# A seven-product block scheme in f32: two of the seven products accumulated in PSUM onto banks of earlier products, in place of two VectorE additions per block pair

## The chip, the cores and the metric

The kernel runs on one core of one Trainium2 chip. The metric is the time of one execution on the device in microseconds (us): the median of three runs of the kernel before is 1294.61 (1294.13 to 1297.48). Lower is better.

## What is computed

One layer of a streaming encoder over 576 tokens (512 of a new stream, 64 of a running one), all in f32: model width 1024, FFN width 2816. What matters here are the matrix products; `W` stands for the weights of each.

```python
x += 0.5 * (silu(h @ W_gate) * (h @ W_up)) @ W_down      # h = rms_norm(x): first FFN, "f1"
p  = rms_norm(x) @ w_in                                  # 7 x 1024 columns
y_a = (B_a * dwconv3(C_a * V_a)) @ w_a_out
y_b = silu(layer_norm(dwconv31(glu(U_b)) + bias)) @ w_b_out
x += (sigmoid(g_a) * y_a + sigmoid(g_b) * y_b) @ w_out
x += 0.5 * (silu(h @ W_gate) * (h @ W_up)) @ W_down      # second FFN, "f2"
y  = rms_norm(x)
```

## The kernel before

**Products.** Tokens lie in the free dimension, in two halves of H = 288 columns. Each f32 operand is split into a high part (rounded to `float32r`) and a low part (the remainder), and a product is the sum of three matmuls: high x high, high x low, low x high. A matmul is 128x128 weights times 128x288 data into one PSUM bank.

**The block scheme.** From a certain column tile on (`PLAIN`: tile 4 of f1, tile 1 of f2; FFN tiles 0 to 21) gate and up are computed together, and so are two of the four pairs of column tiles of `w_b_out`. Such a *pair* is a 2x2 block product: two halves of the 1024 input rows and two column tiles on the weight side, two halves of the tokens and of the rows on the data side. Done plainly that is eight products of 128 columns by 512 rows by 288 tokens; the kernel does it in seven (a scheme of Strassen's kind), on sums and differences of weight halves and of data halves. Each product is 12 matmuls, `block` (L452): four row tiles, three parts each. The data forms are made once (`Forms.operands`, L669); the weight sums are made for each pair. The seven results q[0] to q[6] are then added up into gate and up, four halves in all. There are 41 pairs: 18 in f1, 2 in `w_b_out`, 21 in f2.

**Adding up, before** (`pair`, L863; the same in `block_pair`, L1240). After each product but the first one step is recorded:

```python
            steps = (
                lambda: sca.copy(q1, q[0]),
                lambda: dve.tensor_tensor(u2, q[1], q1, op=ALU.subtract),
                lambda: dve.tensor_tensor(u4, q[2], u2, op=ALU.subtract),
                q7,
                lambda: dve.tensor_tensor(half(t, 0), q[4], q1, op=ALU.add),
                gate,
            )
```

Here `q7` adds u3 = q[3] + u2 and writes the second up half, u3 - q[2]. `gate` adds the second gate half, q[5] + u4, multiplies by the norm's factor and takes ScalarE's SiLU. The last step, q[6] + u3, is recorded beside the next pair's first products. So a pair has one ScalarE copy out of PSUM and seven VectorE operations with a PSUM operand.

**Temporaries.** q1, q[0]'s copy, and u2 are the two halves of one temporary of 576 columns, u3 and u4 those of another (before). A temporary is one tile to the framework that sets the semaphores.

**PSUM.** Four tiles of two banks each (pool `mmps`, L135), 512 f32 to a bank. `bank()` (L164) hands out half a tile at a time, so that two consecutive products share a tile; the other users take whole tiles. A product writes 288 columns of its bank. The half that is left over is dropped at the end of each FFN group (L921) and after each `w_b_out` pair (L1273). Seven products before, five after the change: in both an odd number, so that a pair's first product falls on the first half of a tile in one pair and on the second half in the next.

**Order.** Every instruction is recorded at L88 in the order of the program, and each engine's queue keeps it. FFN column tiles come in four groups (`GROUPS`, L44: tiles 0-4, 5-9, 10-15, 16-21); after each group the down projection of that group's tiles follows. In between go the weight steps of `Stream` (L202), six units ahead of the product that needs them: a load on SyncE's queue, VectorE's sums of weight halves (`add`), ScalarE's high part (`begin`, L280), and the low part either on ScalarE and a GpSimd DMA that accumulates (L284) or by a VectorE subtraction (`end`). `ws.get` ahead of each product calls them, so they stand in the queues ahead of that product's step. In `block_pair` of tiles 6 and 7 the split of two merged tiles is recorded with the fourth step.

Of the kernel before, what the change touches and what calls it, by code (L numbers as in the profile page):

```python
# [13 lines left out]
ALU = mybir.AluOpType  # L14
# [8 lines left out]
KU = KT // 2  # L23
# [88 lines left out]
def tile_encoder_step(  # L112
# [707 lines left out]
    def ffn(f, xg, sums, finish, forms, R=None, todo=()):  # L820
# [42 lines left out]
        def pair(i, hs, last):  # L863
            qu, uu, t, cu = (ttile() for _ in range(4))
            q1, u2, u3, u4 = half(qu, 0), half(qu, 1), half(uu, 0), half(uu, 1)
            q = []

            def q7():
                dve.tensor_tensor(u3, q[3], u2, op=ALU.add)
                dve.tensor_tensor(half(cu, 1), u3, q[2], op=ALU.subtract)  # L870

            def gate():
                dve.tensor_tensor(half(t, 1), q[5], u4, op=ALU.add)
# [11 lines left out]
            for n, xs in enumerate(bs):  # L885
                q.append(block(ws.get(plan[f, "s", i][n]), xs))
                if n > 0:
                    steps[n - 1]()
                if rest:
                    rest.pop(0)()  # L890

            hs.append(None)
            at = len(hs) - 1

            def up():
                if last:
                    dve.tensor_tensor(t, t, R, op=ALU.mult)
                dve.tensor_tensor(half(cu, 0), q[6], u3, op=ALU.add)
# [341 lines left out]
    def block_pair(i):  # L1240
        j = 2 * i
        c1, c2, qu, uu = (ttile() for _ in range(4))
        q1, u2, u3, u4 = half(qu, 0), half(qu, 1), half(uu, 0), half(uu, 1)
        q = []

        def second():
            dve.tensor_tensor(u3, q[3], u2, op=ALU.add)
            dve.tensor_tensor(half(c2, 1), u3, q[2], op=ALU.subtract)

            if i == KU - 1:  # L1250
                MS[4], MS[5] = split(M[4]), split(M[5])

        def first():
            dve.tensor_tensor(half(c1, 1), q[5], u4, op=ALU.add)
# [3 lines left out]
        steps = (  # L1258
# [179 lines left out]
```

## Time and profile before

| | |
|---|---|
| median of three runs | 1294.61 us |
| span of the profiled execution | 1290.1 us |
| TensorE busy | 1279.4 us, 99% of the span, 9728 matmuls |
| VectorE busy | 925.1 us, 72% |
| ScalarE busy | 765.5 us, 59% |
| GpSimd busy | 361.6 us, 28% |
| TensorE's granted clock | 10 tenths in all but the last of the 40 slices |
| chain that ended last | 92% TensorE |

The times come from runs without the profiler's records, the rows from one profiled execution of 1290.1 us; what lies around its span makes the median longer. Rows of a stretch of time give the start and duration in us, the engine, the line, the operation with output and inputs by tile name, the shape, and in brackets how long the engine was idle before it and for whom. All of the kernel's engine instructions bear L88.

### The profile page before, as it was taken

The page shows a single profiled execution, that of the slowest core. Times are in us where ns is not written, and L with a number is a line of the kernel's source. Part 1 is how long each engine was busy: PE and PEld are TensorE (multiplying, and loading weights), DVE is VectorE, ACT ScalarE, POOL GpSimd, SP SyncE. Part 2 cuts the span into 40 slices and gives each one's busy share as a digit, 9 for nine tenths or more (in the row PEclk, how much of TensorE's full clock was granted, in tenths as well). Part 3 has the DMA queues.
Part 4 walks back from the last instruction along what each step waited for, and adds up shares of the span by engine and source line. Part 5 has one row for each costly group of instructions (what it writes and reads, how often), then busy time and mean ns, then how long its engine had stood idle before and what let it go on. Part 6 is the DMA issues. An engine that isn't in the chain of part 4 may idle for free.

```text
span 1290.1 us, 25702 instructions
## 1 busy us (share of the span) xinstructions
PE 1279.4 (99%) x9728; PEld 1277.5 (99%) x9728; DVE 925.1 (72%) x1539; ACT 765.5 (59%) x1359; POOL 361.6 (28%) x460
## 2 busy tenths in 40 slices
PE   9999999999999999999999999999999999999997
PEld 9999999999999999999999999999999999999997
DVE  6868668748846998888895166656867848847956
ACT  7655646646776645555444576477665655654664
POOL 0032332232333444333321221122142141241230
PEclk9999999999999999999999999999999999999998
DMA  7286787886799898788885767696687696796783
GB/s 220 70 181 154 163 180 155 177 181 149 154 224 232 174 200 173 165 172 174 172 172 124 163 142 154 151 236 145 139 175 171 151 197 151 164 204 138 158 172 97
DMA packets 286812, 215.26 MB, mean 167 GB/s; under 512 B 15456, under 2 KB 248928, under 8 KB 286688
## 3 DMA queue, kind: packets, MB, share of 16 engines
q0 software_dynamic: 56160, 92.43, 43.3%
q1 hardware_dynamic: 228784, 120.35, 32.8%
q8 instruction: 77, 1.26, 0.4%
q10 hardware_dynamic: 1744, 0.83, 0.2%
q14 instruction: 47, 0.39, 0.1%
HBM read 116.17 MB, written 4.98 MB: 94 GB/s over the span
## 4 chain that ended last, share of the span: by engine, by line
PE 92%; issue 4%; DVE 2%; DMA 1%; ACT 1%; POOL 0%; DVEq 0%; POOLq 0%; ACTq 0%
PE mm L88 92%; DVE tmp L88 0%; DMA g<-raw 0%; DMA raw<-in_w_b_out_dram 0%; DVE x L88 0%; DVE g L88 0%; DMA u<-raw 0%; ACT act L88 0%; DVE w L88 0%; POOL u L88 0%; DVE act L88 0%; ACT u L88 0%; ACT w L88 0%; ACT g L88 0%; POOL g L88 0%
## 5 line engine op out<-in xcount | busy, mean ns | idle before, releaser
L88 PE MATMUL mm<-act,u 128*128 128x288 f32 x4758 | 668.3, 293 | 0.1
L88 PEld LDWEIGHTS mm<-act,u 128*128 128x128 f32 x4758 | 638.9, 188 | 0.4 <-DMA u<-raw 0.3
L88 PE MATMUL mm<-act,g 128*128 128x288 f32 x3030 | 432.9, 294 | 0.9 <-DMA g<-raw 0.9
L88 PEld LDWEIGHTS mm<-act,g 128*128 128x128 f32 x3030 | 410.3, 188 | 1.1 <-DMA g<-raw 1.1
L88 POOL DMA_DIRECT2D u<-raw x197 | 172.3, 874 | 481.7 <-ACT u L88 317.4
L88 PE MATMUL mm<-act,act 128*128 128x288 f32 (+2 forms) x1896 | 259.9, 293 | 0.0
L88 PEld LDWEIGHTS mm<-act,act 128*128 128x128 f32 x1896 | 252.2, 188 | 0.5 <-ACT act L88 0.3
L88 ACT CAST u<-raw 128x512 fp32r<-128x512 f32 (+2 forms) x207 | 118.8, 574 | 172.0 <-PE mm L88 136.7
L88 POOL DMA_DIRECT2D g<-raw x126 | 109.9, 872 | 297.4 <-ACT g L88 242.7
L88 DVE SCALAR_TENSOR_TENSOR w<-g,prm,w 128x606 f32<-128x606 f32 x232 | 179.3, 844 | 1.4 <-ACT w L88 1.4
L88 DVE TENSOR_TENSOR tmp<-mm,tmp 128x288 f32<-128x288 f32 (+1 forms) x251 | 112.9, 459 | 70.3 <-PE mm L88 53.7
L88 ACT ACTIVATE u<-u 128x512 fp32r<-128x512 f32 (+2 forms) x197 | 116.8, 593 | 6.2
L88 ACT CAST g<-raw 128x512 fp32r<-128x512 f32 (+2 forms) x136 | 75.1, 553 | 43.9 <-DMA raw<-in_ffn_w_down_dram 17.6
L88 DVE SCALAR_TENSOR_TENSOR tmp<-mm,r 128x576 f32<-128x576 f32 x48 | 36.3, 757 | 76.6 <-PE mm L88 76.6
L88 POOL DMA_DIRECT2D act<-raw x67 | 59.1, 883 | 108.3 <-ACT act L88 94.5
L88 ACT CAST act<-tmp 128x576 fp32r<-128x576 f32 x92 | 61.9, 675 | 43.1 <-DVE tmp L88 42.1
L88 ACT CAST g<-w 128x512 fp32r<-128x512 f32 x79 | 49.0, 620 | 64.4 <-DVE w L88 58.6
L88 ACT CAST u<-w 128x512 fp32r<-128x512 f32 x81 | 50.2, 619 | 61.0 <-DVE w L88 43.6
L88 DVE TENSOR_TENSOR act<-tmp,act 128x576 fp32r<-128x576 f32 x92 | 67.5, 754 | 18.1 <-ACT act L88 16.5
L88 ACT ACTIVATE g<-g 128x512 fp32r<-128x512 f32 (+2 forms) x126 | 72.1, 572 | 4.0
L88 DVE TENSOR_TENSOR w<-raw,raw 128x512 f32<-128x512 f32 x82 | 56.2, 685 | 16.2 <-DMA raw<-in_ffn_w_gate_up_dram 11.2
L88 ACT ACTIVATE tmp<-tmp 128x576 f32<-128x576 f32 x47 | 32.2, 686 | 45.1 <-DVE tmp L88 45.0
(86 smaller groups left out, 830.6 us busy)
## 6 DMA issues: line engine op xcount, KB each, us to landing
raw<-in_ffn_w_gate_up_dram SPq DMA_DIRECT2D x171, 256.0 KB, 3.5
u<-raw POOLq DMA_DIRECT2D x140, 256.0 KB, 4.2
raw<-in_w_in_dram SPq DMA_DIRECT2D x112, 256.0 KB, 3.8
raw<-in_ffn_w_down_dram SPq DMA_DIRECT2D x96, 192.0 KB, 3.8
g<-raw POOLq DMA_DIRECT2D x69, 256.0 KB, 4.2
act<-raw POOLq DMA_DIRECT2D x61, 256.0 KB, 4.4
g<-raw POOLq DMA_DIRECT2D x43, 192.0 KB, 4.5
u<-raw POOLq DMA_DIRECT2D x41, 192.0 KB, 4.5
```

Of the source, the lines that this page charges most:

```text
L88: return self.tc.keep_in_program_order(fn(*args, **kwargs))
```

## The change

`block` gets an argument `onto`: a PSUM bank that it adds to (no start flag) instead of a new one. A new function `seven` holds the scheme for both callers. The fifth product (q[4]) accumulates onto q[0]'s bank and the sixth (q[5]) onto q[2]'s (`ONTO`). So the sums q[4] + q[0] and q[5] + q[2] come from TensorE. Since those banks are then overwritten, q[2] is copied by ScalarE first (q3), and the fifth product's sum is copied by ScalarE to the first gate half. VectorE's u4 = q[2] - u2 and its q[4] + q1 go, and the second gate half is now q[5] - u2. A pair has three ScalarE copies and five VectorE operations on PSUM, and takes five banks in place of seven. u3 shares its temporary with q3, the copy, where it shared with u4. The functions that it replaces, and the new ones:

```diff
-    def block(w, xs):
-
-        q = bank()[:, :H]
+    def block(w, xs, onto=None):
+
+        q = bank()[:, :H] if onto is None else onto
...
-                pe.matmul(q, l[:, k, :], r, start=k == m == 0, stop=k == KU - 1 and m == 2)
+                pe.matmul(
+                    q, l[:, k, :], r, start=onto is None and k == m == 0,
+                    stop=k == KU - 1 and m == 2, skip_group_check=onto is not None,
+                )
         return q
+    ONTO = {4: 0, 5: 2}
+
+    def seven(ws7, xs7, c1, c2, gate, between=None):
+        qu, uu = ttile(), ttile()
+        q1, u2, q3, u3 = half(qu, 0), half(qu, 1), half(uu, 0), half(uu, 1)
+        q = []
+
+        def second():
+            dve.tensor_tensor(u3, q[3], u2, op=ALU.add)
+            dve.tensor_tensor(half(c2, 1), u3, q3, op=ALU.subtract)
+
+        def first():
+            dve.tensor_tensor(half(c1, 1), q[5], u2, op=ALU.subtract)
+            gate()
+
+        steps = (
+            lambda: sca.copy(q1, q[0]),
+            lambda: dve.tensor_tensor(u2, q[1], q1, op=ALU.subtract),
+            lambda: sca.copy(q3, q[2]),
+            second,
+            lambda: sca.copy(half(c1, 0), q[4]),
+            first,
+        )
+        for n, xs in enumerate(xs7):
+            q.append(block(ws.get(ws7[n]), xs, q[ONTO[n]] if n in ONTO else None))
+            if n > 0:
+                steps[n - 1]()
+            if between:
+                between()
+        return lambda: dve.tensor_tensor(half(c2, 0), q[6], u3, op=ALU.add)
...
         def pair(i, hs, last):
...
-            steps = (
-                lambda: sca.copy(q1, q[0]),
-                lambda: dve.tensor_tensor(u2, q[1], q1, op=ALU.subtract),
-                lambda: dve.tensor_tensor(u4, q[2], u2, op=ALU.subtract),
-                q7,
-                lambda: dve.tensor_tensor(half(t, 0), q[4], q1, op=ALU.add),
-                gate,
-            )
...
+            final = seven(plan[f, "s", i], bs, t, cu, gate, between)
```

What this makes of the queues is shown at two places. In the first pair of the second FFN, TensorE's queue before has these rows at the start of the fifth product (after the fourth's last matmul, into `mm_11430`) and of the sixth; both go into a new tile, `mm_11470`:

```order
L88 MATMUL mm_11430<-act_11231,u_11252 128x288
L88 MATMUL mm_11470<-act_10740,g_11305 128x288 [waits DVE_49,Activation_49]
L88 MATMUL mm_11470<-act_10741,g_11305 128x288
L88 MATMUL mm_11470<-act_10740,g_11306 128x288 [waits DMASW4_49]
...
L88 MATMUL mm_11470<-act_11208,g_11306 128x288
L88 MATMUL mm_11470<-act_10740,u_11310 128x288 [waits Activation_49]
L88 MATMUL mm_11470<-act_10741,u_11310 128x288
L88 MATMUL mm_11470<-act_10740,u_11310 128x288
```

The same two starts on TensorE after the change, where `mm_11370` is the tile of the first and second products and `mm_11410` that of the third and fourth:

```order
L88 MATMUL mm_11410<-act_11211,u_11232 128x288
L88 MATMUL mm_11370<-act_10720,g_11285 128x288 [waits DVE_49]
L88 MATMUL mm_11370<-act_10721,g_11285 128x288
L88 MATMUL mm_11370<-act_10720,g_11286 128x288 [waits DMASW4_49]
...
L88 MATMUL mm_11370<-act_11188,g_11286 128x288
L88 MATMUL mm_11410<-act_10720,u_11290 128x288 [waits DVE_49]
L88 MATMUL mm_11410<-act_10721,u_11290 128x288
L88 MATMUL mm_11410<-act_10720,u_11290 128x288
```

The fifth product now writes the first product's tile and waits for VectorE, the sixth the third product's tile, again with a wait for VectorE, where before the fifth took a new tile (its waits those of its operands and of that tile) and the sixth waited for ScalarE.

VectorE's queue in the same pair before, from u4 (the row on `mm_11430` that waits for PE) over u3 and the up half to both gate halves; `w`, `u` and `g` are weight steps:

```order
L88 TENSOR_TENSOR tmp_11373<-mm_11430,tmp_11372 128x288 [waits DVE_49,PE_49]
L88 TENSOR_TENSOR u_11451<-w_11377,u_11451 128x512 [waits Activation_49]
L88 TENSOR_TENSOR tmp_11373<-mm_11430,tmp_11372 128x288
L88 TENSOR_TENSOR tmp_11375<-tmp_11373,mm_11430 128x288 [waits DVE_49]
L88 TENSOR_TENSOR g_11468<-w_11447,g_11467 128x512 [waits Activation_49]
L88 TENSOR_TENSOR w_11486<-w_11405,raw_11384 128x512 [waits DMAHW2_49]
L88 TENSOR_TENSOR tmp_11374<-mm_11470,tmp_11372 128x288 [waits PE_49]
L88 TENSOR_TENSOR tmp_11374<-mm_11470,tmp_11373 128x288
```

The same stretch on VectorE after, with u3 the row on `mm_11410` and `tmp_11354`:

```order
L88 TENSOR_TENSOR w_11427<-raw_11226,raw_11049 128x512
L88 TENSOR_TENSOR u_11431<-w_11357,u_11431 128x512 [waits Activation_49]
L88 TENSOR_TENSOR tmp_11355<-mm_11410,tmp_11354 128x288 [waits DVE_49,Activation_49]
L88 TENSOR_TENSOR tmp_11353<-tmp_11355 128x288 [waits DVE_49]
L88 TENSOR_TENSOR g_11448<-w_11427,g_11447 128x512 [waits Activation_49]
L88 TENSOR_TENSOR w_11465<-w_11385,raw_11364 128x512 [waits DMAHW2_49]
L88 TENSOR_TENSOR tmp_11352<-mm_11410,tmp_11354 128x288 [waits PE_49]
```

The row of u4 and the one on q[4] are gone; u3 has a wait for ScalarE (the copy q3) in place of what u4 had, and the second gate half reads q[5] and u2.

In the first block pair of `w_b_out`, VectorE's queue before, from u2 (on `mm_10162`) over u4 to u3 and the half behind it; `w_10231` is a sum of weight halves that needs two loads (the DMAHW waits):

```order
L88 TENSOR_TENSOR tmp_10148<-mm_10162,tmp_10148 128x288 [waits Activation_49]
L88 TENSOR_TENSOR act_10194<-raw_10005,act_10193 128x512 [waits DMAHW0_49,Activation_49]
L88 TENSOR_TENSOR tmp_10149<-mm_10196,tmp_10148 128x288 [waits DVE_49,PE_49]
L88 TENSOR_TENSOR u_10213<-raw_10011,u_10213 128x512 [waits DMASW6_49,DMAHW1_49,DMASW1_49,Activation_49]
L88 TENSOR_TENSOR w_10231<-raw_10158,raw_10160 128x512 [waits DMAHW6_49,DMAHW4_49]
L88 TENSOR_TENSOR tmp_10149<-mm_10196,tmp_10148 128x288
L88 TENSOR_TENSOR tmp_10147<-tmp_10149,mm_10196 128x288 [waits DVE_49]
```

The same on VectorE after, u2 on `mm_10144` and u3 on `mm_10178`:

```order
L88 TENSOR_TENSOR tmp_10130<-mm_10144,tmp_10130 128x288 [waits Activation_49]
L88 TENSOR_TENSOR act_10176<-raw_9987,act_10175 128x512 [waits DMAHW0_49,Activation_49]
L88 TENSOR_TENSOR u_10195<-raw_9993,u_10195 128x512 [waits DMASW6_49,DMAHW1_49,DMASW1_49,Activation_49]
L88 TENSOR_TENSOR w_10213<-raw_10140,raw_10142 128x512 [waits DMAHW6_49,DMAHW4_49]
L88 TENSOR_TENSOR tmp_10131<-mm_10178,tmp_10130 128x288 [waits DVE_49,Activation_49]
L88 TENSOR_TENSOR tmp_10129<-tmp_10131 128x288 [waits DVE_49]
```

Only u4 has gone there; the sum of weight halves still stands ahead of u3. In this pair too the sixth product's first matmul on TensorE waits for VectorE.

More of the change, by code (lines that the diff above doesn't have):

```diff
@@ L897, in up @@
                     dve.tensor_tensor(t, t, R, op=ALU.mult)
-                dve.tensor_tensor(half(cu, 0), q[6], u3, op=ALU.add)
+                final()
             def hidden():
@@ L1241, in block_pair, with between @@
         j = 2 * i
[L1242 to L1251, printed above, removed]
+        c1, c2 = ttile(), ttile()
         def first():
[L1254 removed]
             dve.tensor_tensor(c1, c1, SGB[j], op=ALU.mult)
             merged(j, c1)
[L1258 to L1270 removed]
+        def between():
+            if i == KU - 1 and between.n == 4:
+                MS[4], MS[5] = split(M[4]), split(M[5])
+            between.n += 1
+        between.n = 0
+        seven(plan["yb", "s", i], bs, c1, c2, first, between)()
         dve.tensor_tensor(c2, c2, SGB[j + 1], op=ALU.mult)
```

25 lines of the change are left out of this document (2 added, 23 removed).

## The prediction

> **What bounds the kernel now.** The page's first part comes first, then the chain of waits of TensorE, then stretches of time, to see whether TensorE's pace depends on the other engines.
>
> ```profile
> PE 1279.4 (99%) x9728; PEld 1277.5 (99%) x9728; DVE 925.1 (72%) x1539; ACT 765.5 (59%) x1359; POOL 361.6 (28%) x460
> ```
>
> The waits of TensorE alone, longest first (who waited, for whom, us in total, times, longest):
>
> ```profile
> PE mm L88 <- POOL eps L88: 1.0, 1, 1.0
> PE mm L88 <- DMA g<-raw: 0.9, 1, 0.9
> PE mm L88 <- ACT tmp L88: 0.5, 1, 0.5
> ```
>
> Stretches of 20 us: busy time and count of TensorE, its weight loads, VectorE, ScalarE, GpSimd, then the granted clock:
>
> ```profile
> 440.00:460.00 20.00, 20.00 (x157) 20.00 (x155) 19.97 (x33) 13.37 (x23) 11.52 (x18) 1.00 1.09 226
> ...
> 720.00:740.00 20.00, 20.00 (x156) 20.00 (x156) 1.52 (x2) 6.23 (x11) 3.54 (x5) 1.00 0.85 178
> ...
> 840.00:860.00 20.00, 19.14 (x145) 18.90 (x144) 9.29 (x15) 13.35 (x22) 6.89 (x8) 1.00 1.11 262
> ```
>
> TensorE is never without work for long: its listed waits are 1.0 + 0.9 + 0.5 = 2.4 us of 1290.1. Its pace is the same with VectorE full (157 matmuls in 20 us) and nearly empty (156). So time taken off VectorE can give back only what TensorE now waits for, at most those 2.4 us, while each wait that the change puts in front of a matmul is added in full. The whole question is which waits are new, and how late their releasers are.
>
> **What is removed and added.** Durations of the reads of PSUM (min/median/max in ns):
>
> ```profile
> L88 DVE TENSOR_TENSOR tmp<-mm,tmp x251: 446/451/757, 32.9 to 1244.8; 128x288 f32<-128x288 f32 x123, 128x576 f32<-128x576 f32 x3
> ...
> L88 ACT COPY tmp<-mm x49: 378/382/627, 63.4 to 1234.8; 128x288 f32<-128x288 f32 x41, 128x576 f32<-128x576 f32 x8
> ```
>
> There are 41 pairs (41 copies of 288 columns, one each). Per pair VectorE loses two additions, 2 x 0.45 us, in all 37 us of 925; ScalarE gains two copies, 2 x 0.38, in all 31 us of 765. Neither engine is the bound, so both sums count nothing by themselves. TensorE has the same matmuls in the same order.
>
> The new waits are in the rows of the order: the fifth product must wait until its bank has been read, and so must the sixth. In 23 of the 41 pairs (those whose first product takes the first half of a PSUM tile, the first pair of each group among them) both matmuls name VectorE, not ScalarE. The fifth waits for u2, the difference that reads the second product in the other half of the same tile; the sixth waits for u3, the sum that reads the fourth. The other 18 pairs wait for ScalarE's copies alone. u3 itself stands behind the new copy of the third product (it writes the other half of the same temporary). So I look, in the 23, at when u2 and u3 end against when the products now start.
>
> *First pair of the first FFN.* TensorE's fifth product; then VectorE's u2, the addition that goes (u4), and u3; then ScalarE's copy (start us, us):
>
> ```profile
> 63.17 1.74 PE L88 MATMUL mm<-act,g 128*128 128x288 f32 x12
> ```
>
> ```profile
> 64.95 0.45 DVE L88 TENSOR_TENSOR tmp<-mm,tmp 128x288 f32<-128x288 f32 x1
> ...
> 65.65 0.45 DVE L88 TENSOR_TENSOR tmp<-mm,tmp 128x288 f32<-128x288 f32 x1
> ...
> 66.48 0.45 DVE L88 TENSOR_TENSOR tmp<-mm,tmp 128x288 f32<-128x288 f32 x1
> ```
>
> ```profile
> 63.41 0.39 ACT L88 COPY tmp<-mm 128x288 f32<-128x288 f32 x1
> ```
>
> u2 ends at 65.40 behind other work that the change leaves alone, so the fifth product moves from 63.17 to about 65.44 (0.04 for the signal): +2.27. The sixth would then start at 65.44 + 1.58 = 67.02; u3, with u4's 0.37 gone from its queue, ends by 66.56, so it costs nothing. Term: +2.3.
>
> *First block pair of w_b_out.* TensorE's sixth product; VectorE's u2, the weight sum ahead of u3, and u3:
>
> ```profile
> 816.53 1.75 PE L88 MATMUL mm<-act,g 128*128 128x288 f32 x12
> ```
>
> ```profile
> 813.40 0.45 DVE L88 TENSOR_TENSOR tmp<-mm,tmp 128x288 f32<-128x288 f32 x1
> ...
> 818.56 0.69 DVE L88 TENSOR_TENSOR w<-raw,raw 128x512 f32<-128x512 f32 x1 [2.36 <-DMA raw<-in_w_b_out_dram]
> 819.17 0.45 DVE L88 TENSOR_TENSOR tmp<-mm,tmp 128x288 f32<-128x288 f32 x1
> ```
>
> u2 is early. But ahead of u3 VectorE's queue holds the sum of two weight halves, which waits for a load to land. Today nobody waits for u3; now the sixth product does, and moves from 816.53 to 819.62 + 0.04: +3.1. Nothing in the change brings that load in sooner.
>
> *Second block pair of w_b_out.* TensorE's sixth product and its next wait, and ScalarE's last weight step ahead of the new copy:
>
> ```profile
> 840.15 1.75 PE L88 MATMUL mm<-act,act 128*128 128x288 f32 x12
> ...
> 845.70 1.59 PE L88 MATMUL mm<-act,g 128*128 128x288 f32 x10 [0.86 <-DMA g<-raw]
> ```
>
> ```profile
> 839.28 0.63 ACT L88 ACTIVATE g<-g 128x512 fp32r<-128x512 f32 x1
> ```
>
> The copy of the third product ends near 839.91 + 0.3, u3 0.5 later at 840.7: the sixth product waits 0.6. The load that it waits for at 845.70 is issued from the step that ends at 839.91, so it lands no later, and that wait shrinks by as much. Net 0.
>
> *First pair of the second FFN*, two later starts that run 0.16 and 0.34 longer than their 1.74, and the sixth product of the next of the 23 pairs (938.75, with its u3 at 939.97):
>
> ```profile
> 914.49 1.74 PE L88 MATMUL mm<-act,g 128*128 128x288 f32 x12
> 916.07 1.75 PE L88 MATMUL mm<-act,u 128*128 128x288 f32 x12
> ...
> 919.24 1.90 PE L88 MATMUL mm<-act,u 128*128 128x288 f32 x12
> ...
> 928.91 2.08 PE L88 MATMUL mm<-act,u 128*128 128x288 f32 x12
> ...
> 938.75 1.75 PE L88 MATMUL mm<-act,u 128*128 128x288 f32 x12
> ```
>
> ```profile
> 915.60 0.46 DVE L88 TENSOR_TENSOR tmp<-mm,tmp 128x288 f32<-128x288 f32 x1 [0.70 <-ACT tmp L88]
> ...
> 918.05 0.45 DVE L88 TENSOR_TENSOR tmp<-mm,tmp 128x288 f32<-128x288 f32 x1
> ...
> 919.02 0.45 DVE L88 TENSOR_TENSOR tmp<-mm,tmp 128x288 f32<-128x288 f32 x1
> ...
> 939.97 0.45 DVE L88 TENSOR_TENSOR tmp<-mm,tmp 128x288 f32<-128x288 f32 x1
> ```
>
> ```profile
> 915.19 0.38 ACT L88 COPY tmp<-mm 128x288 f32<-128x288 f32 x1
> ...
> 916.57 0.61 ACT L88 CAST u<-w 128x512 fp32r<-128x512 f32 x1
> ```
>
> The fifth product moves from 914.49 to 916.06 + 0.04: +1.6. The sixth could then start at 917.68; u3, with u4's 0.37 gone, ends at 919.10, so it starts at 919.14: another 1.5, together 3.1. With TensorE that much later the two lengthened products (0.16 + 0.34 = 0.5 us of waiting) find their operands there: +2.6 net. In the next of the 23 pairs u3 ends 1.67 after the sixth product's start today (940.42 against 938.75), and TensorE comes 2.6 later; it doesn't wait.
>
> *The other pairs*, by the fourth pair of the first FFN: its fourth and sixth products; VectorE's sixth-product addition of the pair before, u4 and u3; ScalarE's SiLU and copy:
>
> ```profile
> 126.37 1.74 PE L88 MATMUL mm<-act,g 128*128 128x288 f32 x12
> ...
> 129.53 1.74 PE L88 MATMUL mm<-act,g 128*128 128x288 f32 x12
> ```
>
> ```profile
> 121.84 0.46 DVE L88 TENSOR_TENSOR tmp<-mm,tmp 128x288 f32<-128x288 f32 x1 [0.52 <-PE mm L88]
> ...
> 128.93 0.45 DVE L88 TENSOR_TENSOR tmp<-mm,tmp 128x288 f32<-128x288 f32 x1
> ...
> 129.90 0.45 DVE L88 TENSOR_TENSOR tmp<-mm,tmp 128x288 f32<-128x288 f32 x1
> ```
>
> ```profile
> 123.12 0.69 ACT L88 ACTIVATE tmp<-tmp 128x576 f32<-128x576 f32 x1 [1.46 <-DVE tmp L88]
> ...
> 126.06 0.38 ACT L88 COPY tmp<-mm 128x288 f32<-128x288 f32 x1
> ```
>
> Bound from above: u3 ends at 130.35, 0.82 after the sixth product's start; less u4's 0.37 leaves 0.45 of waiting. Bound from below: the fourth product ends at 128.11; signal 0.04, copy 0.38, signal 0.04, u3 0.45 end at 129.02, 0.5 ahead of the start. I take the lower end, no wait, because the queue moves forward by more than u4: the pair before loses its addition on the fifth product (0.37) and u4 (0.37), and its sixth-product addition no longer waits 0.52 for the seventh, which has another tile now. That is about 1.3 us; SiLU at 123.12 waits for VectorE, and the first copy follows SiLU and four weight steps without a pause, so copy and u2 come some 1 us earlier. The margin of 0.5 is thin, and some ten of the 23 pairs are in this position. The rest have more: the first pairs of groups have TensorE just behind them.
>
> Sum: 2.3 + 3.1 + 0 + 2.6 + 0 = 8.0 us. On the profiled span 1290.1 gives 1298.1; the median of the three runs, 1294.61, stands 4.5 above that span for what lies around it, so the forecast is 1302.6.
>
> **Where the skill bears on it.** The rows of the order make the fifth and sixth products wait for a reader of the neighbouring bank. The Trainium skill, PSUM — Partial Sum Buffer, section "PSUM bank collisions raise a hardware error", asks only that a bank's own users be kept apart ("by bank is the simple version"); by that, ScalarE's copies would be the only waits needed and the sum would be that of the first rival, 1.7 us.
>
> TensorE's longest pause away from its two ends is the 0.86 us before 845.70, and the clock of that stretch reads 1.00; a pause of 3.0 us (816.53 + 0.16 to 819.66) is beyond what the trace shows. The Trainium skill, TensorE: Matmul & The Clock Gate, section "What's actually happening", halves the clock only after an idle window of about 3.4 us; by that rule the pause is just too short.
>
> **The rivals.** (a) *Not slower: only the copies count.* If u2 and u3 were never the last to come, the fifth product of the first FFN's first pair would start at 63.80 + 0.04 (+0.7), those of the second FFN's first pair at 915.61 (+1.1) and, behind the cast at 916.57 (0.61, so to 917.18) and a copy of 0.38, 917.6 (+0.4), less the 0.5 regained: +1.7, or 1296.3. It decides if VectorE's queue at those places runs over 1 us ahead of today's, or the matmuls don't wait for it. Against it: all work ahead of u2 there is untouched. Chance 0.08.
>
> (b) *VectorE's relief wins.* All 2.4 us of TensorE's waits at most, 1292.2. Against it: 1.0 of that is the start, 0.5 the end, and none lies in a pair's additions. Chance 0.03.
>
> (c) *Slower still: the thin margins fail.* If ten pairs wait by the upper bound, six 0.45 and four, which have one more multiplication in VectorE's queue, some 0.7, that is 5.5 more: 1308.1. It decides if u3 comes 0.5 us later than worked out. For it: u3 is 0.82 late today. Chance 0.15.
>
> (d) *The long pause drops the clock.* The first 20 us of the run bound it:
>
> ```profile
> 0.00:20.00 20.00, 18.97 (x123) 18.50 (x124) 12.33 (x23) 14.56 (x27) 0.44 (x6) 1.00 0.92 274
> ```
>
> 123 matmuls instead of some 154 are 31 x 0.13 = 4 us, with the start's own waits in them: at most 1306.6. Chance 0.04.
>
> **How the numbers follow.** The forecast has the remaining 0.70, with its own spread of about 1300 to 1305 (each of the three terms can be off by half a microsecond, and the thin pairs may add one). From 1299.5 to 1308.5 the range holds it, (d) and nearly all of (c); (a) and (b), 0.11, lie below, a part of (c) above. A measurement of this kernel can tell about 0.3%, 3.9 us, from no change: below 1290.7 is faster, above 1298.5 slower. (a) is "same" and (b) nearly so; (c) and (d) are slower. That gives faster 0.02, same 0.10, slower 0.88.
>
> **What would show it.** In the changed profile, TensorE's list of waits gets two or three entries on VectorE's tmp, together near 8 us: before the fifth product of the first pair in each FFN (2.3 and 1.6), before the sixth in the second FFN's first pair (1.5) and in the first block pair of w_b_out (3.1, with VectorE waiting for the w_b_out load). Matmul counts per 20 us stay at 153 to 157 elsewhere, copies of 288 columns rise from 41 to 123, VectorE's busy time falls by about 37 us. I am wrong if TensorE shows no wait on VectorE (then (a)), if the pairs in mid-group show repeated waits of 0.4 us or more (then (c)), or if the granted clock falls after 816 us (then (d)).

## The result

The changed kernel takes 1300.23 us (median of six runs, 1298.25 to 1303.28) against 1294.37 for the kernel before (six runs, 1291.45 to 1297.48). The ratio is 1.0051, 95% interval 1.0034 to 1.0068: 6.6 us slower, between 4.4 and 8.8. The forecast was 1302.6, from 1299.5 to 1308.5. The profiled execution took 1299.37 us with a span of 1297.5, where the forecast had 1298.1.

One thing is needed to read all times below. Executions of one and the same kernel fall into two groups some 4 us apart (the lower and the upper group from here on): of the 23 runs of before that stood beside the first experiments, eleven took 1290.38 to 1291.96 us and twelve 1294.43 to 1296.72. The traces show where that comes from. The first row is TensorE's stretch from 400 to 700 us in the profile of before, the second the same in a kernel that computes this stretch with the same instructions (`old_at_three`, the first experiment below; busy us, count of matmuls, granted clock, share of the DMA engines, GB/s):

```profile
400.00:700.00 300.00, 300.00 (x2309) 1.00 0.83 175
```

```profile
400.00:700.00 300.00, 300.00 (x2281) 1.00 0.82 172
```

TensorE never waits in either, but it does 28 matmuls fewer, 3.7 us' worth. So a median depends on how many runs had which pace, and what an edit costs is read at the places in the trace. The ratios and their intervals below are worked out over all runs of both kernels, so they need not be the ratios of the two medians that stand beside them. The profiles of before and of the changed kernel both have the quicker pace (2309).

The page of the changed kernel and the waits of TensorE in it:

```profile
PE 1279.9 (99%) x9728; PEld 1277.6 (98%) x9728; DVE 897.3 (69%) x1457; ACT 793.8 (61%) x1441; POOL 360.9 (28%) x460
```

```profile
PE mm L88 <- DVE tmp L88: 7.8, 5, 2.5
PE mm L88 <- POOL eps L88: 1.0, 1, 1.0
PE mm L88 <- ACT tmp L88: 0.5, 1, 0.5
```

VectorE is busy 28 us less, ScalarE 28 us more, and the span is 7.4 us longer with the same matmuls. TensorE's list of waits has one new entry: five waits for VectorE, 7.8 us. The wait for `g<-raw` (0.9) is gone. All five lie in four pairs (start, us, matmuls, idle before and for whom; at 61.03 and 816.77 stand the products ahead of two of these waits, the fourth of the first FFN's first pair and the fifth of the first block pair of `w_b_out`):

```profile
61.03 1.74 PE L88 MATMUL mm<-act,u 128*128 128x288 f32 x12
64.89 1.85 PE L88 MATMUL mm<-act,g 128*128 128x288 f32 x12 [2.12 <-DVE tmp L88]
...
816.77 1.74 PE L88 MATMUL mm<-act,u 128*128 128x288 f32 x12
820.97 2.64 PE L88 MATMUL mm<-act,g 128*128 128x288 f32 x12 [2.47 <-DVE tmp L88]
...
846.92 1.85 PE L88 MATMUL mm<-act,act 128*128 128x288 f32 x12 [0.45 <-DVE tmp L88]
...
921.29 1.85 PE L88 MATMUL mm<-act,g 128*128 128x288 f32 x12 [1.56 <-DVE tmp L88]
924.34 1.84 PE L88 MATMUL mm<-act,u 128*128 128x288 f32 x12 [1.20 <-DVE tmp L88]
```

The same two products stood at these times in before:

```profile
61.59 1.74 PE L88 MATMUL mm<-act,u 128*128 128x288 f32 x12
...
814.95 1.74 PE L88 MATMUL mm<-act,u 128*128 128x288 f32 x12
```

Set against the starts that the prediction quotes, each place has its price. Ahead of the first pair this execution is 0.56 us early (61.03 against 61.59), behind the wait 1.72 late (64.89 against 63.17): 2.28 us. The first block pair of `w_b_out` goes from 1.82 late (816.77 against 814.95) to 4.44 late (820.97 against 816.53): 2.62. What comes behind that second pause was not in the sum (stretch, its length, TensorE's busy us, matmuls, granted clock, share of the DMA engines, GB/s):

```profile
818.00:821.00 3.00, 0.53 (x5) 1.00 0.94 238
821.00:824.00 3.00, 3.00 (x15) 0.62 0.38 114
824.00:827.00 3.00, 3.00 (x21) 0.81 0.31 90
```

In the two stretches after the pause TensorE has 15 and 21 matmuls where a stretch of 3 us at full clock has 25, at a granted clock of 0.62 and 0.81. What that costs is read from the starts: the sixth product is 4.44 us late, the product after the seventh 6.07 (825.77 against 819.70). Of these 1.63 us some 0.1 come behind any wait (behind the first pair's, 1.72 late becomes 1.82: 66.58 against 64.76), so the slow clock takes about 1.5 us.

### The profile page after: what moved, and what is told of

The parts are those of the page before. It is cut to its first block, busy times and chain, and to the rows that moved or that the text cites. A ratio compares the mean times of both kernels' runs of the same rounds, so it can differ in the third digit from the quotient of the medians.

```text
span 1297.5 us, 25588 instructions
## 1 busy us (share of the span) xinstructions
PE 1279.9 (99%) x9728; PEld 1277.6 (98%) x9728; DVE 897.3 (69%) x1457; ACT 793.8 (61%) x1441; POOL 360.9 (28%) x460
## 4 chain that ended last, share of the span: by engine, by line
PE 94%; DVE 3%; ACT 1%; issue 1%; DMA 1%; DVEq 0%; ACTq 0%
PE mm L88 94%; DVE tmp L88 1%; DVE act L88 1%; DVE u L88 0%; ACT act L88 0%; DVE w L88 0%; DMA raw<-in_w_b_out_dram 0%; DVE g L88 0%; ACT u L88 0%; DMA gains<-in_params_dram 0%; ACT r L88 0%; ACT w L88 0%; DVE r L88 0%; DVE x L88 0%; ACT tmp L88 0%
## 5 line engine op out<-in xcount | busy, mean ns | idle before, releaser
L88 ACT CAST u<-raw 128x512 fp32r<-128x512 f32 (+2 forms) x207 | 119.1, 575 | 174.2 <-PE mm L88 147.8
L88 DVE TENSOR_TENSOR tmp<-mm,tmp 128x288 f32<-128x288 f32 (+1 forms) x169 | 78.5, 464 | 91.6 <-PE mm L88 66.5
L88 ACT COPY tmp<-mm 128x288 f32<-128x288 f32 (+1 forms) x131 | 53.0, 405 | 40.4 <-PE mm L88 36.5
```

The source lines that it names most:

```text
L88: return self.tc.keep_in_program_order(fn(*args, **kwargs))
```

## The experiments

The theory: the change costs what three pairs wait, because their fifth or sixth product must wait for VectorE's u2 or u3, which stand late in VectorE's queue there; the other 38 pairs cost nothing. The rivals: the added ScalarE copies cost a little in every pair; the margins in mid-group fail; the accumulation itself costs.

**The old way in three pairs.** The first pair of each FFN and the first block pair of `w_b_out` add up as before, the other 38 as after the change.

```diff
-            final = seven(plan[f, "s", i], bs, t, cu, gate, between)
+            final = seven(plan[f, "s", i], bs, t, cu, gate, between, i == PLAIN[f])   # old way if true
-        seven(plan["yb", "s", i], bs, c1, c2, first, between)()
+        seven(plan["yb", "s", i], bs, c1, c2, first, between, i == 1)()
```

> The change in 38 of the 41 pairs; the first pair of each FFN and the first block pair of w_b_out add up as before. Theory: the three pairs carry the whole cost, the other 38 none: span 1290.1 within 0.7 us, time as before. Rival (thin margins or the load of the copies in all pairs): 38/41 of 7.4 us stay, span near 1297.

Measured: 1291.57 us against 1294.43, ratio 0.9994 (0.9980 to 1.0009): no difference. Its two groups lie where those of before lie (1290.39 to 1291.65 and 1294.83 to 1296.01). The profiled execution is one of the upper group, at the slower pace (2281), so its span is 1293.8 and not the 1290.1 that was expected. TensorE's waits away from the ends of the program (the view ends at 930, in the middle of the second row's product):

```profile
844.74 1.85 PE L88 MATMUL mm<-act,act 128*128 128x288 f32 x12 [0.45 <-DVE tmp L88]
...
929.28 0.93 PE L88 MATMUL mm<-act,u 128*128 128x288 f32 x5 [0.50 <-ACT tmp L88]
```

The first is the second block pair of `w_b_out`, as in the changed kernel; at the second, before has no listed wait, but its product runs 0.34 longer there (2.08 us at 928.91). In 38 pairs the change neither costs nor gains anything that shows (by the interval at most 1.2 us of cost or 2.6 of gain): the three pairs carry it, and the 25 us that VectorE is busy less in this kernel (899.7 against 925.1) buy nothing.

**Every pair on the second half of a tile.** The whole change, with the first half of a new tile skipped ahead of each pair. The fifth product's bank then shares its tile with the skipped half, which no product writes, and the sixth's with the second product, which is read long before the sixth.

```diff
         q = []
+        spare.clear()
+        bank()
```

> The whole change, but every pair starts on the second half of a PSUM tile, so that the fifth product's bank shares its tile with the pair before and the sixth's with the second product: the fifth waits for ScalarE's copy of the first product only, the sixth for ScalarE's copy of the third; the seventh shares a tile with the fourth and waits for u3. All the copies stay. Theory: first FFN's first pair +0.7 (copy ends at 63.80 in before), w_b_out +1.5 (the seventh product, 818.11 in before, waits for u3 at 819.62; that pause is too short for the slow stretch), second FFN's first pair +1.1 +0.4 -0.5: sum +3.2, span near 1293.3. Rival (ScalarE's added copies, spread): unchanged, near 1297.5. Rival (the slow clock comes from the transfers there, not the pause): the stretch at 0.62 stays.

Measured: 1297.03 us, ratio 1.0024 (1.0010 to 1.0038), 3.1 us where the theory had 3.2. Part of this agreement is luck: nine of the twelve runs lie in the upper group (1296.72 us and more), and the profiled execution, at the quicker pace (2308), has a span of 1291.5, only 1.4 above that of before and not near 1293.3. TensorE's waits:

```profile
63.35 1.84 PE L88 MATMUL mm<-act,g 128*128 128x288 f32 x12 [0.50 <-ACT tmp L88]
65.39 1.85 PE L88 MATMUL mm<-act,u 128*128 128x288 f32 x12 [0.19 <-ACT tmp L88]
...
819.80 1.86 PE L88 MATMUL mm<-act,act 128*128 128x288 f32 x12 [0.85 <-DVE tmp L88]
...
911.36 1.85 PE L88 MATMUL mm<-act,u 128*128 128x288 f32 x12 [1.12 <-DVE tmp L88]
```

The fifth product of the first pair waits 0.50 for ScalarE where it waited 2.12 for VectorE, with the same copies in the program. At 819.80 it is the seventh product that waits for u3, 0.85 where 1.5 was expected. At 911.36 it is the second product of the second FFN's first pair: it takes a new tile here, which in before the third product took; that wait was not in the theory, which had one of 1.1 at the fifth. The clock from 821 to 824 is 1.00, with the same transfers in the program: the slow clock came with the long pause.

**u3 ahead of the weight steps**, in the first block pair of `w_b_out` alone.

```diff
+            if soon and n == 4:
+                second()
             q.append(block(ws.get(ws7[n]), xs, q[ONTO[n]] if n in ONTO else None))
-            if n > 0:
+            if n > 0 and not (soon and n == 4):
                 steps[n - 1]()
```

> The whole change; in the first block pair of w_b_out alone, u3 and the subtraction behind it are recorded ahead of two weight steps on VectorE (a low part and the sum that waits for a w_b_out load). Theory (u3 was late there because of that load): the pause of 2.47 us before the sixth product goes, and so does the stretch at 0.62 of the clock behind it, since it came from the pause: against the changed kernel -2.6 -1.5 = -4.1, a span near 1293.4, about 1296 by the median; the waits in the first pairs of the two FFNs stay (2.1, 1.6 and 1.2). Rival (u3 is late for another reason, or the load holds something else up as well): TensorE waits near 818 for another engine and the span stays within 1 us of 1297.5.

Measured at the place: as expected. No wait stands near 818 any more, and the matmuls around it run on (fourth, fifth and sixth product; the view ends at 824.5, in the sixth):

```profile
821.12 1.74 PE L88 MATMUL mm<-act,act 128*128 128x288 f32 x12
822.70 1.74 PE L88 MATMUL mm<-act,u 128*128 128x288 f32 x12
824.28 0.43 PE L88 MATMUL mm<-act,g 128*128 128x288 f32 x2
```

The time did not follow: 1299.91 us, ratio 1.0054 (1.0038 to 1.0071), no less than the changed kernel. The trace has two reasons in other places: it had the slower pace (2282 matmuls from 400 to 700 us), and the pause of the first pair was followed by the slow clock here, which it was not in the changed kernel's profile:

```profile
65.03 3.05 PE L88 MATMUL mm<-act,g 128*128 128x288 f32 x12 [1.75 <-DVE tmp L88]
```

That is twelve matmuls in 3.05 us instead of 1.85. To see whether that belongs to the kernel, the same kernel ran again:

> The same kernel as the run with u3 ahead of the weight steps, again. That run lost 1.6 us by a slow stretch behind a pause of 1.75 us at 65 us, and its TensorE had the slower of two paces between 400 and 700 us (2282 matmuls in place of 2309, 3.7 us). If these two belong to the execution and not to the kernel, some executions here come out 4 to 5 us lower, near 1295, and the sites read the same: a pause of about 2.1 or 1.75 us at 65 us, none at 818. If they belong to the kernel, all lie at 1298 to 1302 again.

Measured: 1297.11 us (twelve runs, 1295.56 to 1300.14), ratio 1.0033 (1.0019 to 1.0047). The pace is the quick one now (2309), but the first pair has its slow stretch again:

```profile
65.08 2.64 PE L88 MATMUL mm<-act,g 128*128 128x288 f32 x12 [2.12 <-DVE tmp L88]
```

So the pace belongs to the execution and not to the kernel. Of the 4.1 us that go at the place, some 1.5 come back as slow clock behind the first pair's pause in both profiles of this kernel; why there and not in the one profile of the changed kernel, two traces don't say.

**Both repairs**, the second half of a tile and u3 first.

> Both repairs together: every pair starts on the second half of a tile, and in the first block pair of w_b_out u3 goes ahead of the two weight steps. All 82 added copies stay. Theory: left are the first FFN's first pair (+0.6, the copy of the first product) and the second FFN's first pair (+1.3 at the fourth product, which takes its tile one product sooner, +0.2 at the fifth), less some 0.5 regained: +1.6 against before in places, no wait near 818 and no stretch under full clock. Rival (the accumulation or the copies cost something that no wait shows): 4 us or more.

Measured: 1294.33 us against 1292.43, ratio 1.0014 (1.0000 to 1.0028), 1.8 us. The waits that are left:

```profile
63.69 1.85 PE L88 MATMUL mm<-act,g 128*128 128x288 f32 x12 [0.51 <-ACT tmp L88]
65.73 1.85 PE L88 MATMUL mm<-act,u 128*128 128x288 f32 x12 [0.19 <-ACT tmp L88]
914.29 1.85 PE L88 MATMUL mm<-act,u 128*128 128x288 f32 x12 [0.97 <-DVE tmp L88]
```

They add up to 1.7 us. (The row at 914.29 is the second product, which takes a new tile, and not the fourth that was expected.) With all 82 copies and all accumulation in place, about 5 of the 6.6 us are gone: within the interval, neither costs anything that no wait shows.

**Only the fifth product** on the first's bank; u4 and a bank for the sixth are back, and one bank is skipped behind the seventh, to keep the count odd.

```diff
-    ONTO = {4: 0, 5: 2}
+    ONTO = {4: 0}
-            lambda: sca.copy(q3, q[2]),
+            lambda: dve.tensor_tensor(u4, q[2], u2, op=ALU.subtract),
...
+        bank()
         return lambda: dve.tensor_tensor(half(c2, 0), q[6], u3, op=ALU.add)
```

> Only the fifth product accumulates onto the first's bank; the sixth has a bank of its own again and its addition on VectorE (u4) is back. Theory (three places, waits for VectorE's read of the neighbouring bank): the wait before the fifth product of the first pair of the first FFN (2.1 us in the changed kernel) stays, so does the one in the second FFN's first pair (1.6), the two before sixth products (2.5 and 1.2) go, and with them the stretch at 0.62 of the clock after the 2.5 us. Against the 1290.1 us of before: +2.3 +1.7 -0.5 regained = +3.5, a span near 1293.6. Rival (the cost is ScalarE's added copies, spread over 41 pairs): one copy of two stays, so about half of the 7.4 us stays but with no wait longer than some 0.2 us, span near 1294 without the two long waits.

Measured: 1309.82 us, ratio 1.0128 (1.0107 to 1.0149), four times what either expected. Beside the two waits that the theory named there are thirteen in mid-group, each before a sixth product (the first and the longest):

```profile
121.40 1.85 PE L88 MATMUL mm<-act,u 128*128 128x288 f32 x12 [0.78 <-DVE tmp L88]
...
1126.75 1.85 PE L88 MATMUL mm<-act,u 128*128 128x288 f32 x12 [1.10 <-DVE tmp L88]
```

The edit had made them: in pairs that start on the second half of a tile, the sixth product now got the other half of the fourth's tile, and so waited for u3, with u4 still ahead of u3 on VectorE. The next kernel takes that sharing out by skipping the bank ahead of the sixth product:

```diff
         for n, xs in enumerate(xs7):
+            if n == 4:
+                bank()
```

> As the run with the fifth product alone on the first's bank, but with one bank skipped ahead of the sixth product instead of behind the seventh, so that the sixth never shares a tile with the fourth. Theory: the thirteen waits of 0.74 to 1.10 us before sixth products in that run came from that sharing (a wait for u3, with u4 still in VectorE's queue) and go; the two waits before fifth products stay (1.74 and 1.56 us): +2.3 +1.7 -0.5 = +3.5 against before, about 1298 by the median. Rival (the fifth product's accumulation itself costs in every pair): still over 1305.

Measured: 1297.94 us, ratio 1.0041 (1.0027 to 1.0055). The thirteen waits are gone; two are left, before the fifth products of the first pairs:

```profile
65.02 1.85 PE L88 MATMUL mm<-act,g 128*128 128x288 f32 x12 [2.12 <-DVE tmp L88]
```

```profile
921.29 1.84 PE L88 MATMUL mm<-act,g 128*128 128x288 f32 x12 [1.46 <-DVE tmp L88]
```

Their 3.6 us are the expected 3.5. The ratio says 5.3, with 3.5 at the edge of its interval; the profile has the slower pace (2282), and all six runs lie within 2 us of each other (1297.83 to 1299.44), about where the upper group of before would be with 3.5 us more. So the fifth product's accumulation itself costs nothing that shows.

**Only the sixth product** on the third's bank; the fifth has its own bank again and its VectorE addition is back, with a bank skipped behind the seventh.

> Only the sixth product accumulates onto the third's bank; the fifth has a bank of its own again and its addition on VectorE is back. Theory: the sixth product waits for u3 in all three places. In the first FFN's first pair it would start at 64.75 and u3 ends at 66.56: +1.8; in the first block pair of w_b_out the same pause as in the changed kernel with the slow stretch behind it, +2.6 +1.5; in the second FFN's first pair it would start at 916.07 and u3 ends near 919.10: +3.1, less 0.5 regained. Sum +8.5, a span near 1298.6: one half of the change costs more than both, because the two waits in a pair overlap. Rival (ScalarE's added copies, spread): about half of the 7.4 us, span near 1294.

Measured: 1312.99 us, ratio 1.0153 (1.0130 to 1.0176), 20 us where 8.5 was expected. The waits of the three pairs were there (1.33 in the first FFN), the products behind the waits of 2.41 and 3.03 us ran slow, and one kind of wait was not foreseen (the first two rows are `w_b_out`'s sixth and seventh products, the third the second FFN's first sixth, the last two the sixth and seventh of a pair in mid-group):

```profile
823.39 3.25 PE L88 MATMUL mm<-act,g 128*128 128x288 f32 x12 [2.41 <-DVE tmp L88]
828.80 2.10 PE L88 MATMUL mm<-act,act 128*128 128x288 f32 x12 [2.16 <-DVE tmp L88]
```

```profile
931.99 2.74 PE L88 MATMUL mm<-act,u 128*128 128x288 f32 x12 [3.03 <-DVE tmp L88]
...
1225.36 1.85 PE L88 MATMUL mm<-act,g 128*128 128x288 f32 x12 [0.34 <-DVE tmp L88]
1227.43 1.85 PE L88 MATMUL mm<-act,u 128*128 128x288 f32 x12 [0.22 <-DVE tmp L88]
```

The seventh product shares a tile with the fifth in this layout and waits for the addition that reads the fifth, 2.16 and 1.23 us in the two pairs of `w_b_out` and 0.18 to 0.22 in mid-group. For u3 the row at 1225.36 is the only wait of a mid-group pair in the list. Beside "Only the fifth product" this bears on the thin margin: with u4 still on VectorE thirteen mid-group pairs waited 0.74 to 1.10 us for u3, with u4 gone one pair 0.34, and with the fifth's addition gone as well (the change) none. The three layouts differ in which pairs share a tile, so this is a hint and not a clean series.

**The copies alone.** The kernel before with two more ScalarE copies in each pair.

```diff
-                lambda: dve.tensor_tensor(u4, q[2], u2, op=ALU.subtract),
+                lambda: both_of(lambda: dve.tensor_tensor(u4, q[2], u2, op=ALU.subtract), cu, q[2]),
-                lambda: dve.tensor_tensor(half(t, 0), q[4], q1, op=ALU.add),
+                lambda: both_of(lambda: dve.tensor_tensor(half(t, 0), q[4], q1, op=ALU.add), cu, q[4]),
```

`both_of` runs the step and then copies the bank to a half of `cu` that is written later; `block_pair` has the same.

> The kernel before, with two more ScalarE copies of 288 columns in each pair, of the third and of the fifth product's bank, into a half of the temporary that is written over later; no product is moved. ScalarE gets the load of the change and VectorE loses nothing. Theory: TensorE doesn't wait for either, span 1290 to 1291 and the time of before within 0.3 per cent. Rival (ScalarE's load slows the pairs): 3 to 7 us more.

Measured: 1296.76 us, ratio 1.0027 (1.0013 to 1.0042), 3.5 us more: not what the theory expected. In the trace one wait is new, in the second FFN's second pair, for a weight's low part, which GpSimd starts behind ScalarE's steps (the same product runs 0.34 longer than its neighbours in before, 2.08 us at 928.91):

```profile
935.89 1.58 PE L88 MATMUL mm<-act,u 128*128 128x288 f32 x10 [1.96 <-DMA u<-raw]
```

The rest of its span is the slower pace (2282 matmuls). That ScalarE's load causes the wait is not shown. The low part's transfer takes 5.15 us from issue to landing here (930.69 to 935.84), and 3.82 in before (925.55 to 929.37). That is 1.3 us of the wait. By TensorE's starts (933.50 against 928.91) the issue comes only 0.55 later, and what the profile names ahead of it is TensorE, not ScalarE.

Nor does the edit give ScalarE the load of the change alone. Each added copy is recorded behind VectorE's addition on the same bank and stands behind it: in this pair the copy of the third product starts at 934.16, 0.04 us after that addition has ended (933.67 and 0.45 us), with ScalarE idle for 1.36 us ahead of it. ScalarE's operations on temporaries wait 113 times for VectorE here, 119.1 us in all; in before it is 41 times and 45.0 us, in the changed kernel 52 times and 41.1. The changed kernel, with the same number of copies, has no wait for a weight. Whether the edit makes the slower pace likelier (eight of ten runs took 1296.05 us or more, of which some 2 are the wait; seven of 17 of before beside them took 1293.52 or more) stays open too.

## Why the prediction was right

The time lies in the range, and TensorE's new waits stand at the places that the prediction named and wait for the readers that it named. That the number came so close is in part luck: two steps were wrong, and their errors stood against each other or against gains that no step foresaw.

- *Time taken off VectorE buys nothing.* Shown: 38 pairs with the change and three without took the time of before. (VectorE's busy time fell by 28 us and not by 37: a row on VectorE can start before the one ahead of it has ended, as 819.17 does before 818.56 + 0.69, so an addition of 0.45 us takes less than 0.45 of busy time.)
- *First pair of the first FFN, +2.3.* Measured 2.28, the fifth product waiting for u2. On the second half of a tile it waited 0.50 for ScalarE instead.
- *First block pair of `w_b_out`, +3.1.* Measured 2.62: the weight sum ahead of u3 began at 819.86 with TensorE 1.82 us late, 0.5 earlier than in before by TensorE's count. u3 ahead of it takes the whole wait away.

```profile
819.86 0.69 DVE L88 TENSOR_TENSOR w<-raw,raw 128x512 f32<-128x512 f32 x1 [2.98 <-DMA raw<-in_w_b_out_dram]
820.47 0.45 DVE L88 TENSOR_TENSOR tmp<-mm,tmp 128x288 f32<-128x288 f32 x1
```

- *Second block pair, 0.* A wait of 0.45 us came where 0.6 was forecast, and the wait for `g<-raw` (0.86) left the list. By TensorE's starts the place gains 0.5 us (6.16 late at 844.73 against 838.57, 5.66 late at 856.48 against 850.82).
- *First pair of the second FFN, +2.6.* The two waits are 1.56 and 1.20; 1.6 and 1.5 were forecast, less 0.5. By TensorE's starts the place costs 2.74 (5.08 late at 917.98 against 912.90, 7.82 late at 938.65 against 930.83).
- *The other pairs, 0.* Rival (c) is refuted: no wait of theirs in the list. The margin is the half microsecond of the lower bound. In the pair that the prediction used u3 starts at 130.40 and ends at 130.86, and the sixth product starts at 131.35:

```profile
130.40 0.46 DVE L88 TENSOR_TENSOR tmp<-mm,tmp 128x288 f32<-128x288 f32 x1
```

```profile
131.35 1.74 PE L88 MATMUL mm<-act,g 128*128 128x288 f32 x12
```

  The reason given was that VectorE's queue moves forward by more than u4, so that the first copy comes 1 us sooner. It does: 126.81 here against 126.06 in before, with TensorE 1.82 later (131.35 against 129.53), is 1.07 sooner.

```profile
126.81 0.40 ACT L88 COPY tmp<-mm 128x288 f32<-128x288 f32 x1
```
- *Rival (a), only the copies count:* refuted by the waits; with the tiles laid out so that it holds in the pairs' fifth and sixth products, the time above before fell from 6.6 to 3.1 us.
- *Rival (d), the clock drops, at 0.04.* This step failed. By the prediction's own sign, a granted clock that falls after 816 us, it came true: the clock dropped behind the 2.47 us pause, at a cost of about 1.5 us. The bound of 4 held, but it came from a stretch whose own clock reads 1.00. The prediction leaned on the idle window of about 3.4 us of the Trainium skill, TensorE: Matmul & The Clock Gate, section "What's actually happening"; here a pause of 1.75 us was enough ("u3 ahead of the weight steps"), and the measurement decides.
- *From span to median, 4.5.* Also wrong: the profiled execution of the changed kernel took 1.9 us more than its span. The 4.5 held the difference between a profile at the quicker pace and three runs that all lie in the upper group. Without the lost clock the forecast would have been further above the result; the two errors stood against each other.
- *The sum on the span, 8.0.* Measured 7.4, with the slow clock's share in it. By TensorE's starts against before, the first pair of the first FFN cost 2.4 us, the first block pair 2.6 and, by the clock, 1.6 more (the 0.1 behind the wait included), the second block pair gave back 0.5, and the second FFN's first pair cost 2.7. The other 1.6 us were gained in three stretches without any wait: 0.56 before the first pair, 0.56 from 856 to 913 us, 0.45 behind the second FFN's first pair. In the second of these the two executions had different paces (last section). No step of the prediction foresaw either amount; that they cancel is luck.

No version was measurably faster than the kernel before: what is left to gain there is 2.4 us of TensorE's waits, and no addition of the block scheme is on that path.

## What to carry to other kernels

Where one engine is busy for 99% of the span, an edit that relieves another engine is worth at most the bound engine's waits; look first at what the bound engine must newly wait for, and at who stands ahead of that in its queue. In the change such waits hung on the few places where stages meet (a stage's first pair, a load landing late), not on the average pair; but a shift of half a tile and one addition more on VectorE ("Only the fifth product") put them into thirteen ordinary pairs as well. When a buffer is written again sooner, the unit in which the framework tracks it counts: two banks to a tile made matmuls wait for a reader of the neighbouring bank, and skipping half a tile brought the cost from 6.6 to 3.1 us by the runs, and the span from 1297.5 to 1291.5 in the two profiles at the quicker pace. And a price for each place is not yet a price for the whole: a long wait can cost more than its length, by the clock behind it.

## What the runs showed of the hardware

**A pause of TensorE can halve its clock well below 3 us, and not always.** Seven pauses, each made of a small matmul, a chain of small VectorE operations and a matmul that reads its end, were put into the kernel before (`pause(n)`, n operations more than the first, after products between 700 and 785 us):

```diff
         product(("p", 5, j), xg, ga_of(j))
+        if PAUSES[j][0] is not None:
+            pause(PAUSES[j][0])
...
+    PAUSES = [(None, None)] * 4 + [(None, 2), (4, 6), (7, 8), (9, 10)]
```

> The kernel before, with seven pauses of TensorE put into the stretch from about 710 to 755 us, where VectorE is nearly idle: a small matmul, a chain of small VectorE operations on its result (3, 5, 7, 8, 9, 10, 11 of them), and a small matmul that reads the end of the chain. It asks what pause brings the slow stretch (0.62 of the clock over 3 us behind a pause of 2.47 us in the changed kernel, none behind 2.12 us). If the length of the pause decides, there is a length between 2.1 and 2.5 us from which each pause is followed by matmuls at 240 ns in place of 131, some 1.5 to 2 us in all, and none below. If what TensorE did before or the transfers decide, long and short pauses here are followed by the same pace.

Measured: 1319.94 us in a single run. Two of the seven, each with the 24 matmuls behind it:

```profile
738.82 0.43 PE L88 MATMUL mm<-dial,tmp 128*128 128x64 f32 x2 [2.13 <-DVE dial L88]
739.07 4.94 PE L88 MATMUL mm<-act,act 128*128 128x288 f32 x24
...
760.74 0.43 PE L88 MATMUL mm<-dial,tmp 128*128 128x64 f32 x2 [2.65 <-DVE dial L88]
760.98 3.42 PE L88 MATMUL mm<-act,act 128*128 128x288 f32 x24
```

Twenty-four matmuls take 3.3 us at full pace; behind 2.13 us of pause they took 4.94, behind 2.65 us 3.42. In all, 2.13, 2.38, 2.41 and 2.90 were followed by a slow stretch, 1.35, 1.87 and 2.65 were not. So length alone doesn't decide. The second run had all seven alike:

> The kernel with seven pauses again, all seven of the same length now, about 2.4 us. In the first such run pauses of 2.13, 2.38, 2.41 and 2.90 us were followed by the slow stretch, those of 1.35, 1.87 and 2.65 us were not. If the length alone decides, all seven are followed by the same pace. If it also depends on where the pause falls against something that runs on by itself (windows of fixed length in which the share of work is counted), some are and some are not; with windows of 3.4 us and a limit at half of them, estimated from the Trainium skill's page TensorE: Matmul & The Clock Gate, section What's actually happening, about five of seven are.

Measured: 1327.06 us in a single run. The first pause became 4.22 us, since VectorE was still at other work, and was followed by a slow stretch. The other six were 2.38 or 2.39, and four of them were followed by one too. Two of the six, one without and one with:

```profile
738.67 0.43 PE L88 MATMUL mm<-dial,tmp 128*128 128x64 f32 x2 [2.38 <-DVE dial L88]
738.92 3.37 PE L88 MATMUL mm<-act,act 128*128 128x288 f32 x24
...
748.01 0.69 PE L88 MATMUL mm<-dial,tmp 128*128 128x64 f32 x2 [2.39 <-DVE dial L88]
748.47 6.10 PE L88 MATMUL mm<-act,act 128*128 128x288 f32 x24
```

The granted clock behind these two (length, busy us, matmuls, granted clock, share of the DMA engines, GB/s):

```profile
738.90:741.90 3.00, 3.00 (x25) 1.00 1.02 239
748.50:751.50 3.00, 3.00 (x14) 0.50 0.49 85
```

Equal pauses, 25 and 14 matmuls in the next 3 us. That fits something that runs on by itself and counts work in windows. The Trainium skill, TensorE: Matmul & The Clock Gate, section "What's actually happening", says of the window in which TensorE's activity is counted that it is free-running. An estimate from the 3.4 us that the same section of the Trainium skill gives the window: a limit at half a window (1.7 us) would fit every pause seen here. The shortest with a slow stretch behind it was 1.75 us; the longest without one was 2.65, which can fall across two windows. No run tested the limit itself.

**Two paces.** TensorE without a wait does 2309 or about 2282 matmuls in 300 us at a granted clock that reads 1.00 in both, 130 or 131.5 ns each, in different executions of the same kernel. In these two profiles the difference lies from 400 to 800 us: there before does 770 or 771 matmuls in 100 us and `old_at_three` 761 to 763, while from 100 to 400 us both do 760 to 765. Both paces also occur inside one execution. In the changed kernel's profile 24 matmuls take 3.32 us at one place and 3.28 at another, and such groups start 3.16 and 3.12 us apart:

```profile
835.26 3.32 PE L88 MATMUL mm<-act,g 128*128 128x288 f32 x24
...
872.08 3.28 PE L88 MATMUL mm<-act,u 128*128 128x288 f32 x24
```

In before it is the other way round at the second place: 3.16 us apart from 857.14 to 891.90, and 3.12 from 901.91 on. What sets the pace, the runs don't show.
